# Attention scores of four tiles at once in every second step, with two tiles in one PSUM bank for each head

## The chip, the cores and the metric

The kernel runs on one NeuronCore of a Trainium2 chip. Its time is device time in microseconds (us). TensorE (PE) multiplies matrices and writes only into PSUM, which has eight banks of 512 float32 columns in each of 128 partitions. VectorE (DVE) and ScalarE (ACT) read PSUM; GpSimd (POOL) works on SBUF alone; SyncE (SP) issues most of the DMAs. Each engine works through its own queue of instructions in order and waits on semaphores for the others.

## The reference, cut to what matters

One decoder block on 1024 tokens of width 1024, in float32: a SwiGLU half-step, a mixer, and another SwiGLU half-step. The change touches the attention of the mixer, which has 12 heads of width 64 in three groups of four, with windows and dilations (128, 1), (512, 4) and (2048, 16):

```python
s = jnp.einsum('brnqhd,brnkhd->brnhqk', qb, kk).astype(jnp.float32) * (Dh ** -0.5)
s = jnp.where(allowed[None, None, :, None], s, -jnp.inf)
m = jnp.max(s, axis=-1, keepdims=True)
p = jnp.exp(s - m)
l = jnp.sum(p, axis=-1, keepdims=True)
o = jnp.einsum('brnhqk,brnkhd->brnqhd', p, vv.astype(jnp.float32)) / jnp.swapaxes(l, 3, 4)
```

Beside attention the mixer has a pooling branch, whose last product is `y_pool @ w_branch_pool` (512 by 1024), and both branches are gated and merged.

## The kernel before, in words

Float32 products are made of three products of rounded parts (high by high, high by low, low by high), the parts being held as `fp32r`.

Attention works on 48 **slots**. A slot is one tile of 128 queries of one group for a pair of heads. Each of the six uses (a group for a pair of heads) has eight slots. A slot has either 128 keys (one block) or 256 keys (two blocks); every slot of the group with dilation 16 has one block, in the group with dilation 4 every second slot has one, in the first group only the first slot has one. The order of the uses is: group 0, 1, 2 for the first pair of heads, then 1, 2, 0 for the second.

The main loop has 24 steps, `q` from 0 to 23; step `q` starts two slots, 2q and 2q+1. So steps 0 to 3 and 20 to 23 belong to the first group, 4 to 7 and 12 to 15 to the second, 8 to 11 and 16 to 19 to the third. The loop is under a manual schedule: each engine executes its instructions in the order in which the code writes them. In step `q` the code writes, in this order:

- `scores` (matmuls on line 1552, written tile `s`): for each slot six matmuls, three products for each of two heads. A head contracts over 64 rows, the first head on partitions 0 to 63 and the second on 64 to 127, so these use half of the array each, and two run side by side. Each slot takes two PSUM banks of the tag `mm`, one for each head.
- `trans_p(q - 1)` (L1599, tile `tp`): PE transposes the exponentials of the step before, 128 by 128 at a time: four to eight transposes for two slots, into one or two banks of the tag `acc`.
- `next(fill)` (L1702, tile `yp`): each call issues four 512-column matmuls of the pooling branch; twelve make one output bank (`acc`). The loop has 38 calls from step 2 on: two in a step, and one where `q % 4 == 3`. The two first calls stand in step 1.
- `gather` (L1650): DVE copies the attention output of step q - 3 out of PSUM.
- `masked` (L1570, tile `e`): DVE adds the mask to the scores and finds the maximum: one instruction for each head of each slot, then one that reads the maximum out.
- `values(q - 2)` (L1632, tile `o`): 6 to 12 matmuls of 256 columns that multiply transposed exponentials with values, into one `acc` bank.
- `split_p(q - 1)`: ACT copies the transposed exponentials to the high part (L1611, `ehi`), DVE makes the low part (L1614, `elo`).
- `split_ring` (L1212 on ACT, L1213 on POOL): the queries and keys of the next use are split into high and low parts. Two of these stand in the third step of a use, one in its second and one in its fourth; in the first use two stand in the third and two in the fourth; in the last use and in the first step of each use there is none.
- `end_branches` (L1716): DVE takes a finished pooling bank.
- `exponents` (L1579): ACT takes the exponentials in place, four instructions with an accumulator read after each.
- `house`: DMAs of statistics and values, and late side work.

In steps 18 to 21 the code also transposes weighting factors (`fa`, L1533, banks of the tag `mm`) between `masked` and `values`. PSUM is one pool with four banks of each tag, `mm` and `acc`. The framework gives a bank to a new tile when the instructions that use its old tile are done, and keeps two engines off the same bank at the same time: a reader of a bank waits for the matmuls into it that were written earlier in the code.

Of the kernel before, what the change touches and what calls it, by code (L numbers as in the profile page):

```python
# [16 lines left out]
P = 128  # L17
# [8 lines left out]
HD = 64  # L26
SC = HD ** -0.5
GROUPS = 3
# [8 lines left out]
def tokens(g, i):  # L37

    if g == 0:
        return i * P, 1, (i - 1 if i > 0 else None)  # L40
    if g == 1:
        r, b = divmod(i, 2)
        return r + 4 * P * b, 4, (i - 1 if b else None)
    return i, 8, None
# [74 lines left out]
def three(hi_lo_l, hi_lo_r):  # L119

    lh, ll = hi_lo_l
    rh, rl = hi_lo_r
    return ((lh, rh), (lh, rl), (ll, rh))
# [3 lines left out]
def tile_block(  # L127
# [29 lines left out]
    ve, ac, gp, pe = nc.vector, nc.scalar, nc.gpsimd, nc.tensor  # L157
# [10 lines left out]
    def bank(tag, name):  # L168
        return psum.tile([P, HALF], F32, tag=tag, name=name)
# [1028 lines left out]
    ring = {}  # L1198

    def load_ring(u, tile):  # L1200

        ring[u] = []
        for a in range(2):
            y, hi = tile(F32, f"qk{u}_{a}_in"), tile(F32R, f"qk{u}_{a}_hi")
            nc.sync.dma_start(y, qk_dram[u][a].rearrange("h d c -> (h d) c"))
            ring[u].append((hi, y.bitcast(F32R), y))

    def split_ring(u, n):

        hi, lo, y = ring[u][n // 2]  # L1210
        c = (LOWS, HIGHS)[n % 2]
        ac.activation(hi[:, c], y[:, c], AF.Copy)  # L1212
        gp.tensor_tensor(lo[:, c], y[:, c], hi[:, c].bitcast(F32), op=OP.subtract)  # L1213
# [24 lines left out]
    def load_branch(d):  # L1238
        w, gb = row_part(f"wab{d}"), row(f"gb{d}")
        nc.sync.dma_start(w.rearrange("p (q c) -> p q c", q=2).bitcast(F32), late_w[1 + d][:, :, 256:768])  # L1240
        nc.sync.dma_start(gb, gate_dram[d][:, 1])
        pool_in[d] = (w.rearrange("p (q c) -> p q c", q=2), gb)
# [116 lines left out]
    with tc.manual_schedule():  # L1359
# [4 lines left out]
        for k in range(len(items) + 4):  # L1364
# [6 lines left out]
            if k < len(items):  # L1371
                q, m = items[k]
# [3 lines left out]
            if k - 1 in results:  # L1376
                q, m = items[k - 1]
# [40 lines left out]
    def open_w_o():  # L1418
        wo_pools.append(wo.enter_context(sbuf(f"wo{len(wo_pools)}", "right")))
# [46 lines left out]
    slots = [(hp, g, i) for hp in range(HPAIRS) for g in ((0, 1, 2), (1, 2, 0))[hp] for i in range(NT)]  # L1466
# [30 lines left out]
    def make_factors(hp, eng):  # L1497
        st = stats[hp]
        m, l = st[:, :, :, 0:2], st[:, :, :, 2:4]
        top = att_small.tile([P, 1, NT, 2], F32, name=f"top{hp}")  # L1500
        w = att_small.tile([P, GROUPS, NT, 2], F32, name=f"w{hp}")
        f = att_small.tile([P, GROUPS, NT, 2], F32, name=f"f{hp}")
        every = [P, GROUPS, NT, 2]
        ve.tensor_tensor(top[:, 0], m[:, 0], m[:, 1], op=OP.min)
        ve.tensor_tensor(top[:, 0], top[:, 0], m[:, 2], op=OP.min)
        eng.tensor_tensor(w, top.to_broadcast(every), m, op=OP.subtract)
        yield
        ac.activation(w, w, AF.Exp)
        yield
        eng.tensor_tensor(f, w, l, op=OP.mult)  # L1510
        eng.tensor_tensor(top[:, 0], f[:, 0], f[:, 1], op=OP.add)
        eng.tensor_tensor(top[:, 0], top[:, 0], f[:, 2], op=OP.add)
        ve.reciprocal(top, top)
        eng.tensor_tensor(f, w, top.to_broadcast(every), op=OP.mult)

        f_of[hp] = sums_o.tile([P, GROUPS, NT * 2, HD], F32, tag="f", bufs=1, name=f"f_of{hp}")
        for g in range(GROUPS):
            src = f[:, g].rearrange("p i a -> p (i a)")[:, :, None].to_broadcast([P, NT * 2, HD])
            if hp == 0:
                gp.tensor_copy(f_of[hp][:, g], src)  # L1520
            elif g == 1:
                ve.tensor_copy(f_of[hp][:, g], src)
            else:
                ac.activation(f_of[hp][:, g], src, AF.Copy)
        yield
# [10 lines left out]
    def blocks(g, i):  # L1536

        return 1 if tokens(g, i)[2] is None else 2

    T = {}  # L1540

    def scores(s):
        hp, g, i = slots[s]
        u = hp * GROUPS + g
        n = blocks(g, i)
        ks = slice((i + 1 - n) * P, (i + 1) * P)
        ps = [bank("mm", f"s{s}_{a}")[:, :n * P] for a in range(2)]
        (qhi, qlo, _), (khi, klo, _) = ring[u]
        for j, (l, r) in enumerate(three((qhi, qlo), (khi, klo))):
            for a in range(2):  # L1550
                rows = slice(a * HD, (a + 1) * HD)
                pe.matmul(ps[a], l[rows, i * P:(i + 1) * P], r[rows, ks], start=(j == 0), stop=(j == 2))  # L1552
        T[s] = {"s": ps}

    def masked(s):
        hp, g, i = slots[s]
# [34 lines left out]
    def trans_p(q):  # L1591
        tiles, n = pair(q)
        banks = [bank("acc", f"tp{q}_{j}") for j in range(-(-n // HALF))]
        tp[q] = []
        for s, c0, w in tiles:
            p = banks[c0 // HALF][:, c0 % HALF:c0 % HALF + w] if n <= HALF else banks[s % 2][:, :w]
            e = T[s].pop("e").rearrange("p a c -> p (a c)")
            for j in range(w // P):
                pe.transpose(p[:, j * P:(j + 1) * P], e[:, j * P:(j + 1) * P], ident)  # L1599
            tp[q].append((p, c0, w))  # L1600
        if n <= HALF:
            tp[q] = [(banks[0][:, :n], 0, n)]
# [120 lines left out]
    def send():  # L1723
        while stores:
            nc.sync.dma_start(*stores.pop())

    def branches():
        for n in range(2 * KT):
            yield from branch(n)

    fill = branches()
# [45 lines left out]
    def advance(gen, n=1):  # L1777
        for _ in range(n):
            next(gen, None)
# [24 lines left out]
    with tc.manual_schedule():  # L1804
        load_ring(uses[1], ring_tile)
        load_branch(1)
        factors = [make_factors(hp, eng) for hp, eng in enumerate((gp, ve))]
        combines = [[Combine(hp, half, adds, lower) for half in range(2)]
                    for hp, (adds, lower) in enumerate((((gp, gp), gp), ((gp, ve), ve)))]
        splits = {}  # L1810
        for q in range(N // 2):
            send()
            u, i = divmod(q, NT // 2)
            if 0 < u < len(uses) - 1 and i == 0:
                load_ring(uses[u + 1], ring_tile)
            scores(2 * q)
            scores(2 * q + 1)
            if q == 1:
                next(fill)
                next(fill)  # L1820
            if q > 0:
                trans_p(q - 1)
                splits[q - 1] = split_p(q - 1)
            if q > 1:
                next(fill, None)
                if q % 4 != 3:
                    next(fill, None)
            if q > 2:
                gather(2 * q - 6)
                gather(2 * q - 5)  # L1830
            masked(2 * q)
            masked(2 * q + 1)

            j = q - N // 4 - 6
            fa = [combines[0][j // 2]] * (2 - j % 2) if 0 <= j < 4 else []
            for f in fa:
                f.rows()
            if q > 1:
                values(q - 2)
            if q > 0:  # L1840
                advance(splits[q - 1], 2)
            for n in ((), (0,) if u > 0 else (), (2, 1) if u > 0 else (0, 2), (3,) if u > 0 else (1, 3))[i]:
                if u + 1 < len(uses):
                    split_ring(uses[u + 1], n)
            for f in fa:
                f.product()
            end_branches()
            exponents(2 * q)
            exponents(2 * q + 1)
            house(2 * q)  # L1850
            house(2 * q + 1)
        send()
        right_b.close()
        load_ya(3)
        load_merge(0)
        load_merge(1)
        open_w_o()
        q = N // 2
        trans_p(q - 1)
        splits[q - 1] = split_p(q - 1)  # L1860
        advance(factors[1])
        next(fill, None)
        values(q - 2)
        gather(2 * q - 6)
        gather(2 * q - 5)
        advance(splits[q - 1], 2)
        advance(factors[1], 2)
        next(fill, None)
        end_branches()
        values(q - 1)  # L1870
        for s in range(2 * q - 4, 2 * q):
            gather(s)
        for n in range(8):
            combines[1][n // 4].step()
            if n != 3:
                next(fill, None)
            end_branches()
            send()
            if n == 3:
                load_merge(2)  # L1880
        for k in (3, 4):
            load_merge(k)
# [34 lines left out]
    ops, banks = {}, {}  # L1917
# [66 lines left out]
    with tc.manual_schedule():  # L1984
# [66 lines left out]
        r = [rows_first2(t) for t in range(2)]  # L2051
# [211 lines left out]
```

## Time and profile before

| | |
|---|---|
| median of three runs | 1911.03 us (1910.6 to 1911.14) |
| the profiled execution, own time | 1910.72 us |
| its span | 1908.9 us |
| mean granted TensorE clock | 0.999 |
| PE busy | 99% of the span |
| the attention loop in the profile | about 1044.5 to 1147.4 us |

In a timeline the columns are the start in us, the length in us, the engine, the line, the operation, what it writes and reads, shapes and how many instructions are merged into the row; in brackets stands how long the engine sat idle before and what released it. In the chain of waits a piece begins where the piece before it ended. The matmuls overlap in the pipeline, so the rate of PE is read from the starts of matmuls, not from their lengths.

### The profile page before, as it was taken

To read this page: it belongs to the slowest core of one execution; us is meant where nothing else is said; L and a number is where in the kernel's file an instruction comes from. 1 tells how busy PE (TensorE), PEld (TensorE's weight loads), DVE (VectorE), ACT (ScalarE), POOL (GpSimd) and SP (SyncE) were. 2 spreads that over 40 slices of the span, in tenths; PEclk is the share of its full clock that TensorE was granted. 3 is DMA by queue.
4 is the path that set the end of the run, shared out by engine and by line. 5 is a ranking of instruction groups with operands and counts; after the bars stand their busy time and mean duration, and the time that the engine had idled before them with its cause. 6 is when DMAs were issued, how large, how long until landed. Compare 5 with 4: busy or idle time off the path is not lost.

```text
span 1908.9 us, 24939 instructions
## 1 busy us (share of the span) xinstructions
PE 1896.3 (99%) x8946; PEld 1574.4 (82%) x8946; DVE 1336.5 (70%) x2017; ACT 760.1 (40%) x1364; POOL 732.0 (38%) x548
## 2 busy tenths in 40 slices
PE   9999999999999999999999999999999999999998
PEld 8888888888888887888888888888888888888886
DVE  7786556557776776667875896887665556577777
ACT  6333333333344543334444772353333323333344
POOL 6333333331223355454544455553333333312132
PEclk9999999999999999999999999999999999999999
DMA  4155223336466627655667977643433223454564
GB/s 189 50 194 176 83 88 106 138 116 208 150 234 217 204 92 228 230 215 195 235 223 286 292 247 270 262 152 119 169 116 127 84 88 116 150 192 139 193 221 166
DMA packets 144940, 331.98 MB, mean 174 GB/s; under 512 B 19120, under 2 KB 39856, under 8 KB 143280
## 3 DMA queue, kind: packets, MB, share of 16 engines
q1 hardware_dynamic: 137280, 308.00, 46.9%
q10 hardware_dynamic: 7536, 22.39, 3.2%
q8 instruction: 70, 1.15, 0.3%
q14 instruction: 54, 0.44, 0.1%
HBM read 229.61 MB, written 100.73 MB: 173 GB/s over the span
## 4 chain that ended last, share of the span: by engine, by line
PE 91%; issue 3%; POOL 2%; DVE 2%; ACT 1%; DMA 1%; SPq 0%; POOLq 0%; ACTq 0%; DVEq 0%
PE d_f L754 18%; PE u_mixm L332 16%; PE wo L1954 4%; PE yp L1702 2%; PE o L1632 1%; PE ya L1767 1%; PE s L1552 1%; PE u_f20b L332 1%; PE u_f11a L332 1%; PE u_f20a L332 1%; PE u_f11b L332 1%; PE u_f210b L332 1%; PE u_f210a L332 1%; PE u_f29b L332 1%; PE u_f29a L332 1%
## 5 line engine op out<-in xcount | busy, mean ns | idle before, releaser
L754 PE MATMUL d_f<-bhi_f,ahi_f 128*128 128x512 f32 x616 | 240.4, 390 | 0.0
L754 PE MATMUL d_f<-bhi_f,alo_f 128*128 128x512 f32 x616 | 239.8, 389 | 0.0
L754 PE MATMUL d_f<-blo_f,ahi_f 128*128 128x512 f32 x616 | 239.7, 389 | 0.0
L716 POOL TENSOR_TENSOR alo_f<-g_f,ahi_f 128x512 fp32r<-128x512 f32 x60 | 84.3, 1421 | 293.6 <-ACT ahi_f L712 293.6
L332 PE MATMUL u_mixm<-xhi_t_mix,wc_mixm 128*128 128x512 f32 x608 | 195.2, 392 | 1.2 <-POOL wc_mixm L309 1.1
L332 PE MATMUL u_mixm<-xhi_b_mix,wc_mixm 128*128 128x512 f32 x456 | 148.9, 392 | 0.0
L754 PEld LDWEIGHTS d_f<-bhi_f,alo_f 128*128 128x128 f32 x616 | 115.6, 188 | 24.7 <-DVE alo_f L716 0.4
L332 PEld LDWEIGHTS u_mixm<-xhi_t_mix,wc_mixm 128*128 128x128 f32 x608 | 113.7, 188 | 26.8 <-POOL wc_mixm L309 2.7
L754 PEld LDWEIGHTS d_f<-blo_f,ahi_f 128*128 128x128 f32 x616 | 115.7, 188 | 23.8
L754 PEld LDWEIGHTS d_f<-bhi_f,ahi_f 128*128 128x128 f32 x616 | 115.6, 188 | 23.7 <-DVE xlo_b_mix L411 0.2
L332 PE MATMUL u_mixm<-xlo_t_mix,wc_mixm 128*128 128x512 f32 x304 | 118.4, 389 | 0.0
L309 POOL TENSOR_TENSOR wc_mixm<-s_mixm,wc_mixm 128x512 fp32r<-128x512 f32 x52 | 73.5, 1414 | 101.8 <-ACT wc_mixm L304 101.8
L332 PEld LDWEIGHTS u_mixm<-xhi_b_mix,wc_mixm 128*128 128x128 f32 x456 | 85.6, 188 | 17.7 <-issue 0.3
L304 ACT ACTIVATE wc_mixm<-s_mixm 128x512 fp32r<-128x512 f32 x76 | 47.3, 628 | 125.7 <-DVE s_mixm L364 56.7
L332 PE MATMUL u_mixm<-xlo_b_mix,wc_mixm 128*128 128x512 f32 x228 | 88.8, 389 | 0.0
L712 ACT ACTIVATE ahi_f<-g_f 128x1024 fp32r<-128x1024 f32 x84 | 81.9, 975 | 4.1 <-DMA g_f<-gs_f 4.1
L309 POOL TENSOR_TENSOR wc_mixm<-raw,wc_mixm 128x512 fp32r<-128x512 f32 x40 | 61.0, 1529 | 44.6 <-ACT wc_mixm L304 33.3
L712 ACT ACTIVATE bhi_f<-s_f2w 128x512 fp32r<-128x512 f32 x55 | 32.7, 627 | 96.0 <-DVE s_f2w L732 88.4
L332 PEld LDWEIGHTS u_mixm<-xlo_t_mix,wc_mixm 128*128 128x128 f32 x304 | 57.1, 188 | 11.8
L712 ACT ACTIVATE bhi_f<-s_f1w 128x512 fp32r<-128x512 f32 x55 | 32.9, 630 | 85.1 <-DVE s_f1w L732 80.3
L716 DVE TENSOR_TENSOR alo_f<-g_f,ahi_f 128x1024 fp32r<-128x1024 f32 (+1 forms) x48 | 58.6, 1222 | 7.8 <-ACT ahi_f L712 7.8
L1954 PE MATMUL wo<-w_o,o_hi 128*128 128x512 f32 x224 | 60.2, 391 | 0.0
(1321 smaller groups left out, 5077.6 us busy)
## 6 DMA issues: line engine op xcount, KB each, us to landing
g_f<-gs_f SPq DMA_DIRECT2D x70, 512.0 KB, 4.8
gs_f<-y_f SPq DMA_DIRECT2D x88, 256.0 KB, 3.3
raw<-in_w2a_dram SPq DMA_DIRECT2D x35, 512.0 KB, 3.9
raw<-in_w2b_dram SPq DMA_DIRECT2D x35, 512.0 KB, 4.2
gs_f<-gb_f SPq DMA_DIRECT2D x46, 256.0 KB, 2.3
raw<-in_w1a_dram SPq DMA_DIRECT2D x22, 512.0 KB, 4.8
raw<-in_w3a_dram SPq DMA_DIRECT2D x22, 512.0 KB, 5.6
raw<-in_w1b_dram SPq DMA_DIRECT2D x22, 512.0 KB, 4.3
```

The costliest lines, as they stand in the source:

```text
L304: ac.activation(w[:, 0], src, AF.Copy)
L309: eng.tensor_tensor(w[:, 1], src, w[:, 0].bitcast(F32), op=OP.subtract)
L332: pe.matmul(p, a, b, start=(start and i == 0), stop=(i == 11), skip_group_check=not start)
L712: ac.activation(hi[:, c], src, AF.Copy)
L716: eng.tensor_tensor(lo[:, d], src[:, o], hi[:, d].bitcast(F32), op=OP.subtract)
L754: pe.matmul(self.banks[m][t], l, r, start=(first and q == 0), stop=(last and q == 2))
L1552: pe.matmul(ps[a], l[rows, i * P:(i + 1) * P], r[rows, ks], start=(j == 0), stop=(j == 2))
L1632: pe.matmul(p, l, r, start=(j == 0), stop=(j == end))
L1702: pe.matmul(p, a, b, start=(j == 0), stop=(j == 11))
L1767: pe.matmul(p, a, b, start=(j == 0), stop=(j == 5))
L1954: pe.matmul(banks[m][t], l, r, start=(st == 0 and n == 0), stop=(st == 1 and n == 5))
```

## The change

Scores are now issued only in even steps: `scores(q)` and `scores(q + 1)`, which is the work for slots 2q to 2q + 3. One call takes two `mm` banks, one for each head, and both of its slots lie side by side in them, each in its half of 256 columns. Odd steps issue no scores. The pooling calls are shared out otherwise: from step 2 on, an even step has one, an odd step has two, and steps 5, 9, 13, 17 and 21 have a third one, at the end, after `values` and the split. The number of calls in the loop stays 38. Nothing else moves.

```diff
-    def scores(s):
-        hp, g, i = slots[s]
-        u = hp * GROUPS + g
-        n = blocks(g, i)
-        ks = slice((i + 1 - n) * P, (i + 1) * P)
-        ps = [bank("mm", f"s{s}_{a}")[:, :n * P] for a in range(2)]
-        (qhi, qlo, _), (khi, klo, _) = ring[u]
-        for j, (l, r) in enumerate(three((qhi, qlo), (khi, klo))):
-            for a in range(2):
-                rows = slice(a * HD, (a + 1) * HD)
-                pe.matmul(ps[a], l[rows, i * P:(i + 1) * P], r[rows, ks], start=(j == 0), stop=(j == 2))
-        T[s] = {"s": ps}
+    def scores(q):
+
+        banks = [bank("mm", f"s{q}_{a}") for a in range(2)]
+        for s in (2 * q, 2 * q + 1):
+            hp, g, i = slots[s]
+            u = hp * GROUPS + g
+            n = blocks(g, i)
+            ks = slice((i + 1 - n) * P, (i + 1) * P)
+            c0 = s % 2 * 2 * P
+            ps = [b[:, c0:c0 + n * P] for b in banks]
+            (qhi, qlo, _), (khi, klo, _) = ring[u]
+            for j, (l, r) in enumerate(three((qhi, qlo), (khi, klo))):
+                for a in range(2):
+                    rows = slice(a * HD, (a + 1) * HD)
+                    pe.matmul(ps[a], l[rows, i * P:(i + 1) * P], r[rows, ks], start=(j == 0), stop=(j == 2))
+            T[s] = {"s": ps}
...
-            scores(2 * q)
-            scores(2 * q + 1)
+
+            if q % 2 == 0:
+                scores(q)
+                scores(q + 1)
...
                 next(fill, None)
-                if q % 4 != 3:
+                if q % 2 == 1:
                     next(fill, None)
...
             if q > 0:
                 advance(splits[q - 1], 2)
+            if q > 1 and q % 4 == 1:
+                next(fill, None)
```

## The prediction

> **What bounds the kernel now.** I read the page first, then the attention loop in stretches of 10 us, then who waits there, then the timeline of single steps. In the fence: the span and the engines' busy time from the page, one stretch of the loop (busy us of each engine, granted clock, DMA share, GB/s), and two of the waits (total us, times, longest).
>
> ```profile
> span 1908.9 us, 24939 instructions
> ...
> PE 1896.3 (99%) x8946; PEld 1574.4 (82%) x8946; DVE 1336.5 (70%) x2017; ACT 760.1 (40%) x1364; POOL 732.0 (38%) x548
> ```
> ```profile
> 1084.00:1094.00 10.00, 10.00 (x77) 8.67 (x76) 9.12 (x38) 6.93 (x23) 6.14 (x5) 1.00 0.98 195
> ```
> ```profile
> ACT ehi L1611 <- PE tp L1599: 19.7, 20, 2.1
> ...
> PEld tp L1599 <- ACT e L1579: 1.5, 5, 0.5
> ```
>
> The reader should see that PE is never idle in this stretch and runs at full clock, so PE time that is saved or lost in the loop counts one for one. DVE comes close behind. ACT has room on average, but it waits 19.7 us for transposes: its work hangs on when PE delivers them. PE in turn waits only 1.5 us for exponentials. The change alters that relation.
>
> **What it saves: passages between full and half array.** The timeline of PE in step 11, where two score matmuls (one for each head) make a row, and two places for comparison from the end of the loop and behind it:
>
> ```profile
> 1091.34 0.28 PE L1632 MATMUL o<-ehi,v_in 128*128 128x256 f32 x1
> ...
> 1091.71 0.28 PE L1552 MATMUL s<-qk_in,qk_hi 64*128 64x128 f32 x2
> ...
> 1092.15 0.28 PE L1552 MATMUL s<-qk_hi,qk_in 64*128 64x128 f32 x2
> 1092.36 0.66 PE L1599 MATMUL tp<-ident,e 128*128 128x128 f32 x4
> ...
> 1147.32 0.28 PE L1632 MATMUL o<-ehi,v_in 128*128 128x256 f32 x1
> 1147.44 1.20 PE L1599 MATMUL tp<-ident,e 128*128 128x128 f32 x8
> ...
> 1153.52 0.60 PE L1533 MATMUL fa<-ident,f_of 128*128 128x128 f32 x4
> ```
>
> From the last value matmul to the first transpose it is 1.02 us with scores between (1091.34 to 1092.36), and 0.12 without (1147.32 to 1147.44). Four transposes take 0.66 behind scores and 0.60 behind pooling. So the scores of a step cost 1.02 - 0.12 + 0.06 = 0.96 us. Appended to another block of scores they cost six pairs at their pitch, (1092.15 - 1091.71) / 4 = 0.11, so 0.66. Each odd step saves 0.30. There are eleven from step 3 on (steps 0 and 1 have their scores back to back already): 3.3 us. I add 0.2 for the scores of step 21, which are stretched today in the stretch with `fa`: **3.5 us saved**.
>
> **The opening.** PE and ACT in the first steps:
>
> ```profile
> 1046.45 0.73 PE L1552 MATMUL s<-qk_hi,qk_hi 64*128 64x256 f32 x2
> ...
> 1049.01 0.19 ACT L1579 ACTIVATION_READ_ACCUMULATOR e<-e,stats 128x1 f32 x1
> ...
> 1049.30 0.82 PE L1599 MATMUL tp<-ident,e 128*128 128x128 f32 x6
> ...
> 1051.29 1.91 PE L1599 MATMUL tp<-ident,e 128*128 128x128 f32 x8 [0.27 <-ACT e L1579]
> ...
> 1052.53 0.19 ACT L1579 ACTIVATION_READ_ACCUMULATOR e<-e,stats 128x1 f32 x1
> ```
>
> The stretched score row (0.73) waits for a bank that `masked` empties; with four banks for four slots, the first two steps wait for none. The last row pair shows the price of a wait on exponentials: the transposes end 1053.20, which is 0.48 after the exponentials (1052.72), because the last head's two transposes follow them. So the transposes of step 0 could end 1049.20 + 0.48 = 1049.68 in place of 1050.12: 0.4 gained, and no more, as the exponentials don't move. Those of step 1 wait anyway, eight in 1.91; the scores of step 3, six pairs or 0.7, now fall into that wait. **1.1 us saved.**
>
> **What it costs: the cover of the exponentials.** In an even step ACT's queue holds: copy of the transposes of step q - 1, the ring splits, exponentials of step q. The copy waits for the transposes of q - 1, which stand behind two blocks of scores now. From the end of those transposes PE has one pooling call and `values` before it needs the exponentials of q; before, it had two pooling calls, `values` and a block of scores. ACT's rows of steps 10, 6, 2 and 16 (the last row of each is the end of its exponentials), and the chain of waits, whose pooling pieces start where transposes end:
>
> ```profile
> 1089.10 0.60 ACT L1611 ACTIVATE ehi<-tp 128x512 fp32r<-128x512 f32 x1 [1.17 <-PE tp L1599]
> 1089.62 1.15 ACT L1212 ACTIVATE qk_hi<-qk_in 128x512 fp32r<-128x512 f32 x2
> ...
> 1092.12 0.19 ACT L1579 ACTIVATION_READ_ACCUMULATOR e<-e,own_stats 128x1 f32 x1
> ```
> ```profile
> 1075.46 0.19 ACT L1579 ACTIVATION_READ_ACCUMULATOR e<-e,own_stats 128x1 f32 x1
> ```
> ```profile
> 1056.65 0.19 ACT L1579 ACTIVATION_READ_ACCUMULATOR e<-e,stats 128x1 f32 x1
> ```
> ```profile
> 1114.80 0.19 ACT L1579 ACTIVATION_READ_ACCUMULATOR e<-e,own_stats 128x1 f32 x1
> ```
> ```profile
> 1053.20 1.85 PE yp L1702 x8
> ...
> 1072.22 1.83 PE yp L1702 x8
> ...
> 1109.20 0.92 PE yp L1702 x4
> 1110.12 1.07 PE o L1632 x9
> ...
> 1112.81 1.85 PE yp L1702 x8
> ...
> 1146.17 1.43 PE o L1632 x12
> ```
> ```profile
> 1089.06 1.84 PE yp L1702 x8
> 1090.90 0.71 PE o L1632 x6
> ```
>
> From the end of the transposes of q - 1 to the end of the exponentials of q, with two ring splits: step 10 1092.31 - 1089.06 = 3.25, step 6 1075.65 - 1072.22 = 3.43, step 2 1056.84 - 1053.20 = 3.64. Without a split: step 16 1114.99 - 1112.81 = 2.18, so the pair of splits costs 1.07, and other steps without one take 2.36 (second group) and 2.57 (first).
>
> The cover is 0.92 plus values, less 0.16 (a piece ends 0.28 after its last start, the transposes could start 0.12 after it): 1.47 with six value matmuls, 1.83 with nine, 2.19 with twelve. To it comes the length of the transposes themselves (0.60 for four; 0.82 for six; eight at 0.11 and 0.27 for the last make 1.03), and the exponentials' end plus 0.48 (0.33 where the last head has one transpose) has to fit in. The idle time of PE is the excess:
>
> - step 10: 3.25 + 0.33 - 1.47 - 0.60 = 1.5
> - steps 6 and 14: 3.43 + 0.48 - 1.83 - 0.82 = 1.3 each; step 2: 3.64 + 0.48 - 1.83 - 1.03 = 1.3
> - step 18: as 10, less eight `fa` transposes at 0.11: 0.6
> - step 12: 2.36 + 0.48 - 1.47 - 0.82 = 0.55; step 22: 0.2; steps 8 and 16: 0.1 each; 4 and 20: none.
>
> Together **6.8 us lost**. This falls on TensorE, and everything behind the transposes in its queue moves with it. After an odd step no such wait arises: two or three pooling calls, values and two blocks of scores stand there, at least 1.84 + 0.71 + 0.96 + 0.66 = 4.2 us, against at most 3.25 in the group with so few value matmuls. DMAs and the queues of SP and POOL keep their order; no DMA is moved past another.
>
> **Banks for the values.** In odd steps the transposes (two banks), a finished and a new pooling bank and the values want five of four `acc` banks in step 13 and in step 23, and in 21 for the late call. PE then waits for DVE's low part. DVE in step 14 and the last scores of that step:
>
> ```profile
> 1102.93 1.62 DVE L1650 COPY o<-o 64x128 f32<-64x128 f32 x4 [0.40 <-PE o L1632]
> 1104.58 0.29 DVE L1570 CUSTOM_DVE_ANT_0 e<-s,mask 128x128 f32<-128x128 f32 x1
> ...
> 1105.70 1.02 DVE L1614 TENSOR_TENSOR elo<-tp,ehi 128x256 fp32r<-128x256 f32 x2
> ```
> ```profile
> 1103.50 0.28 PE L1552 MATMUL s<-qk_hi,qk_in 64*128 64x256 f32 x2
> ```
>
> In step 13 DVE frees the first bank about 1.62 + 1.12 + 0.5 (half of the low part) = 3.2 after the values before; PE asks for it after the wait 0.55, transposes 0.6 and two calls 1.84, so at 3.0: 0.2 to 0.3. In step 23 masks and low parts are longer and DVE runs behind: 0.8; in step 21 0.2. I take **1.3 us lost**; the ends are 0 (a bank happens to be free) and 4 (three times until the pooling bank is taken, the low part's 1.02 and more).
>
> **A rule on shared banks.** In the rows just shown, DVE copies outputs until 1104.55, while the step's scores have all started by 1103.50; so DVE's first mask wouldn't start earlier if half of the scores were enough for it. The Trainium skill, in "PSUM — Partial Sum Buffer", section "PSUM bank collisions raise a hardware error", says that two engines must not touch the same bank and quadrant at once, whatever the addresses, so the first slot's mask has to wait for the second slot's scores in that bank. By the rows this costs nothing; by the rule without that cover it is the last rival below.
>
> **The sum.** 6.8 + 1.3 - 3.5 - 1.1 = +3.5 us on the profiled execution's 1910.72, so 1914.2; the median of the runs shown is 0.31 higher: 1914.5. A measurement can tell about 0.2%, here 3.8 us, from no change, so the forecast lies just inside of that bound, with its own range of +1.5 to +6 on both sides of it.
>
> **The rivals.**
> - *The waits don't add up.* While PE waits for exponentials, DVE catches up; then banks are free, and the other small stretched places near `fa` go too: 6.8 - 3.5 - 1.1 - 0.5 = +1.7, so 1912.7. For it: DVE has 0.9 us of 10 idle in the stretch shown. Against it: its waits would have to be where PE's are.
> - *The chain of ACT stays hidden, and the kernel gets faster.* Then only 3.5 + 1.1 remain: 1906.4. It needs 1.3 us more cover in steps 2, 6, 10, 14, or exponentials that don't queue behind the splits; it is decided where the transposes of an even step's slots start without an idle time of PE. For it: PE waits only 1.5 us on exponentials today. Against it: four rows of ACT in a row, in program order, leave no room.
> - *Shared banks bind.* If DVE is free when an even step's scores begin, its mask starts three pairs of each head later, 0.34 us, and the exponentials with it, in twelve even steps: +4.1 on the forecast, 1918.6. It decides itself where the copies (1.62) end before the scores (1.0). Against it: they end later in every step whose rows I read.
>
> **How the numbers follow.** Forecast 0.45, and I split it by the bound as 0.24 slower and 0.21 within it; waits that don't add up 0.25 (within); shared banks 0.20 (slower); hidden chain 0.10 (faster). This gives faster 0.10, within 0.2% 0.46, slower 0.44. The predicted time is the forecast's 1914.5. The range 1909.5 to 1919 leaves out the hidden chain and waits larger than all bounds above.
>
> **What would show it.** Right: PE idle 1.2 to 1.5 us in front of or within the transposes at the start of steps 3, 7, 11 and 15, released by ACT's exponentials, about 7 us in all over 1.5 now; the passage from values to transposes 0.12 in odd steps; scores in blocks of 24 without stretched rows. Wrong: no such idle time; waits of PE for DVE in the score rows; or waits for a bank in front of values that come near those for exponentials.

## The result, and the profile after

The changed kernel takes 1915.07 us (median of 14 runs, 1914.48 to 1915.9) against 1911.03 (14 runs): a ratio of 1.0022, with a 95% interval from 1.0016 to 1.0029. That is 4.0 us slower, inside the range, 0.6 us above the predicted 1914.5, and just on the slow side of the bound of 0.2%. The profiled execution took 1915.86 us with a span of 1913.8, at the same granted clock of 0.999. From the first score matmul to the first matmul behind the loop (`ya`) PE takes 121.0 us, before 117.2, so 3.8 us are lost there. The two profiled executions differ by 4.9 us in span; the other 1.1 lie outside of that stretch, where the code is the same, and the profiled execution of the changed kernel is one of the slowest of its 14.

After the change: the engines' busy time from the page, and three of the waits in the attention loop, two of PE's weight loads (PEld) and one of its matmuls (total us, times, longest):

```profile
PE 1897.0 (99%) x8946; PEld 1572.6 (82%) x8946; DVE 1337.0 (70%) x2017; ACT 759.7 (40%) x1364; POOL 731.2 (38%) x548
```
```profile
PEld tp L1603 <- ACT e L1583: 7.2, 23, 0.7
...
PEld fa L1533 <- DVE stats L1574: 0.9, 1, 0.9
...
PE tp L1603 <- ACT e L1583: 1.0, 4, 0.5
```

The work is the same, but the transposes wait for exponentials 7.2 us on the weight loads, before 1.5, and 1.0 us on the matmuls, before 0.3 (the two overlap in time and don't add up). The waits for DVE's masks in front of `fa` are new. None of this shows in the page's 99%, for one of its 40 slices is 48 us long and has a 9 as long as PE idles less than 4.8 us in it. The windows view tells more; this is the stretch that the prediction showed as wholly busy:

```profile
1084.00:1094.00 10.00, 9.36 (x67) 7.50 (x67) 8.55 (x36) 6.22 (x22) 5.06 (x5) 1.00 1.00 197
```

The timelines of PE and of ACT of the changed kernel around the end of step 10:

```profile
1091.56 0.28 PE L1636 MATMUL o<-ehi,v_in 128*128 128x256 f32 x1
1092.31 1.48 PE L1603 MATMUL tp<-ident,e 128*128 128x128 f32 x4 [0.47 <-ACT e L1583]
1093.55 0.48 PE L1706 MATMUL yp<-xhi_b_mix,wab 128*128 128x512 f32 x1
```
```profile
1090.24 0.60 ACT L1615 ACTIVATE ehi<-tp 128x512 fp32r<-128x512 f32 x1 [2.81 <-PE tp L1603]
1090.74 1.14 ACT L1212 ACTIVATE qk_hi<-qk_in 128x512 fp32r<-128x512 f32 x2
1091.78 0.39 ACT L1583 ACTIVATE e<-e,own_stats 128x128 f32<-128x128 f32 x1
...
1093.22 0.19 ACT L1583 ACTIVATION_READ_ACCUMULATOR e<-e,own_stats 128x1 f32 x1
```

ACT sits idle for 2.81 us, because the transposes it copies stand behind 24 score matmuls; then it runs copy, two ring splits and four exponentials in a row, and PE, which has only one pooling call and six value matmuls meanwhile, waits. The four transposes of step 11 take 1.48 us, one for each head as its exponentials end, where 0.60 would do, and they start 0.75 us after the last value matmul in place of 0.12.

Three more waits of the changed kernel's PE, two for masks in front of `fa`, one for a bank:

```profile
1126.86 0.85 PE L1533 MATMUL fa<-ident,f_of 128*128 128x128 f32 x6 [0.65 <-DVE own_stats L1574]
```
```profile
1135.66 1.09 PE L1533 MATMUL fa<-ident,f_of 128*128 128x128 f32 x8 [0.47 <-DVE stats L1574]
```
```profile
1150.48 0.39 PE L1636 MATMUL o<-ehi,v_in 128*128 128x256 f32 x1 [0.36 <-DVE elo L1618]
```

From the spacing of PE's starts beyond the usual pitch I read the waits from step 3 on:

| wait of PE | predicted, us | measured, us |
|---|---|---|
| transposes for exponentials of steps 2, 6, 10, 12, 14 | 1.3, 1.3, 1.5, 0.55, 1.3 | 1.05, 1.15, 1.46, 0.48, 1.15 |
| the same, steps 8, 16, 18, 22 | 0.1, 0.1, 0.6, 0.2 | 0.06, 0.06, 0, 0.21 |
| `fa` for masks, steps 18 and 20 | none | 0.81, 0.64 |
| banks: steps 13, 21, 23 | 0.25, 0.2, 0.8 | 0.34, 0.27, 0.53 |
| sum | 8.1 | 8.2 |

(The predicted entries add up to 8.2; 8.1 is the sum that the prediction used. Behind each wait for a bank the next start is another 0.1 late, which the table leaves out.) The loop grew by 3.8, so some 4.4 us came back, 4.6 by the prediction. The table shows sizes, not causes. The runs below test those.

### The profile page after: what moved, and what is told of

Read it like the earlier page. It is cut to its first block, busy times and chain, and to the rows that moved or that the text cites. A ratio compares the mean times of both kernels' runs of the same rounds, so it can differ in the third digit from the quotient of the medians.

```text
span 1913.8 us, 24948 instructions
## 1 busy us (share of the span) xinstructions
PE 1897.0 (99%) x8946; PEld 1572.6 (82%) x8946; DVE 1337.0 (70%) x2017; ACT 759.7 (40%) x1364; POOL 731.2 (38%) x548
## 3 DMA queue, kind: packets, MB, share of 16 engines
q8 instruction: 70, 1.15, 0.2%
```

## Experiments

Each was timed beside the kernel before; ratios are to it.

**The scores alone.** The pooling calls are shared out as before, so an even step has two again.

```diff
                 next(fill, None)
-                if q % 2 == 1:
+                if q % 4 != 3:
                     next(fill, None)
...
-            if q > 1 and q % 4 == 1:
-                next(fill, None)
```

> The change with the pooling calls shared out as before (two in an even step, one or two in an odd one). Cover theory: the second call of the even step adds 0.92 us of cover, so the waits for exponentials in the changed kernel's odd steps (1.05, 1.15, 1.46, 0.48, 1.15 us in steps 3, 7, 11, 13, 15) shrink to about 0.1, 0.2, 0.5, 0, 0.2, and the waits of the factor transposes for masks (0.8 and 0.6) go; about 1.9 us of waits stay against 4.6 saved: 1908.3 us, faster than the kernel before by 0.1%. Shared-bank theory (DVE's masks wait for the scores of the second slot in the bank): the sharing out changes nothing, 1914 to 1916. Theory that the passages saved nothing: about 1911 to 1913.

1910.74 us, ratio 1.0000 (0.9991 to 1.0009). One more pooling call in an even step takes the whole loss away, as the cover theory says and the shared-bank theory doesn't. But the gain to 1908.3 failed to come. The waits of steps 3, 7 and 15 shrank to 0.2 each, as expected; that of step 11 rose to 1.9. ACT's timeline of this kernel in step 10 shows why:

```profile
1087.89 0.60 ACT L1615 ACTIVATE ehi<-tp 128x512 fp32r<-128x512 f32 x1 [1.75 <-PE tp L1603]
1089.77 1.15 ACT L1212 ACTIVATE qk_hi<-qk_in 128x512 fp32r<-128x512 f32 x2 [1.28 <-DMA qk_in<-qk]
1090.82 0.39 ACT L1583 ACTIVATE e<-e,own_stats 128x128 f32<-128x128 f32 x1
```

The ring split waits 1.28 us for its load, which SP issued at 1079.0 to 1080.2; and the exponentials wait behind the split. In the kernel before the same split came at 1089.62 without a wait: there SP issued the load 1.0 us later (1079.99), and it was still on time, so it took at least 1.1 us less. Why it is slower here isn't shown; the next large load on SP's queue (`wab`) is issued 2.6 us after it, in the kernel before 3.9. The other half of the missing gain is waits for DVE from step 18 to step 23, about 2 us, where the expectation leaves 0.9 for all waits other than those for exponentials.

**The pooling calls alone.** The kernel before with the calls of the change.

```diff
                 next(fill, None)
-                if q % 4 != 3:
+                if q % 2 == 1:
                     next(fill, None)
...
+            if q > 1 and q % 4 == 1:
+                next(fill, None)
```

> The kernel before with only the pooling calls shared out as in the change. Cover theory: in an even step the cover of the exponentials is one call, values and a block of scores; by the rows of before this is too short by 0.55 us in step 10, 0.3 in 6 and 14 and 0.2 in step 2: +1.3 us, 1912.3, and up to 1913.5 if banks for values are short in odd steps too. If the sharing out costs nothing by itself: 1911.0.

1913.62 us, ratio 1.0014 (1.0005 to 1.0023). Sharing out is a loss by itself, a little above the range that was expected (1912.3 to 1913.5). In the trace the waits for exponentials are about 1.0 us, a bank in step 13 costs 0.3, and `fa` and the scores behind it lose about 1.8 us to waits for DVE, where the scores of the kernel before lose 0.4.

**Ring splits behind the exponentials**, in the changed kernel and in the kernel with the scores alone:

```diff
-            for n in ((), (0,) if u > 0 else (), (2, 1) if u > 0 else (0, 2), (3,) if u > 0 else (1, 3))[i]:
-                if u + 1 < len(uses):
-                    split_ring(uses[u + 1], n)
...
             exponents(2 * q + 1)
+            for n in ((), (0,) if u > 0 else (), (2, 1) if u > 0 else (0, 2), (3,) if u > 0 else (1, 3))[i]:
+                if u + 1 < len(uses):
+                    split_ring(uses[u + 1], n)
```

> The changed kernel with the ring splits moved behind the exponentials of their step on ACT's and POOL's queues. Cover theory: two splits cost 1.07 us of the chain, so the waits in steps 3, 7, 11, 15 fall to about 0, 0.1, 0.4, 0.1; the 0.5 of step 13, the waits of the factor transposes (1.4) and those for banks (1.3) stay: 1911 us, with 1910 and 1912 as ends. Shared-bank theory: the exponentials wait for the masks and not for the splits, so at most a few tenths: 1914.5 or more.

> Scores of four slots in every second step, pooling calls as before and ring splits behind the exponentials. Cover theory: no wait for exponentials is left after the opening, and what remains is the passages saved (3.5 us) and the opening (1.1) less some 0.5 us of waits for banks: 1906.9 us, 0.2% faster than before. If the passages saved nothing: 1910 to 1911. Shared-bank theory: above 1911.

The changed kernel falls to 1911.75, ratio 1.0005 (0.9997 to 1.0014): 3.3 us of its loss hang on where the ring splits stand. The move takes two of them from in front of the exponentials in each of five even steps, and one or two in nine odd steps; a shared bank has no part in that. With the scores alone it is 1911.64, ratio 1.0004 (0.9995 to 1.0012), 4.7 us more than expected. The waits for exponentials are nearly gone, as expected (0.5 us in step 13 stay). In their place stands one of 1.9 us in front of `fa` in step 18. Timelines of this kernel: PE at `fa`, then DVE from the end of step 17, then POOL:

```profile
1123.65 0.52 PE L1533 MATMUL fa<-ident,f_of 128*128 128x128 f32 x3 [1.75 <-DVE own_stats L1574]
```
```profile
1121.07 0.25 DVE L1513 RECIPROCAL top<-top 128x16 f32<-128x16 f32 x1 [2.67 <-POOL top L1512]
1121.24 1.51 DVE L1654 COPY o<-o 64x128 f32<-64x128 f32 x4
1122.78 0.29 DVE L1574 CUSTOM_DVE_ANT_0 e<-s,mask 128x128 f32<-128x128 f32 x1
```
```profile
1118.91 1.28 POOL L1213 TENSOR_TENSOR qk_in<-qk_in,qk_hi 128x512 fp32r<-128x512 f32 x1 [1.62 <-ACT qk_hi L1212]
1120.15 0.29 POOL L1510 TENSOR_TENSOR f<-w,stats 128x48 f32<-128x48 f32 x1
```

POOL's half of the ring split in step 17 now waits for ACT's later half, the sums of the factors stand behind it on POOL, DVE's reciprocal waits 2.67 us for them, and the copies and masks of step 18 stand behind the reciprocal. The same wait in front of `fa` is in the changed kernel with the splits behind (1.94 us). The move was right for the even steps and wrong for step 17.

**Only in even steps**, in the kernel with the scores alone:

```diff
-            for n in ((), (0,) if u > 0 else (), (2, 1) if u > 0 else (0, 2), (3,) if u > 0 else (1, 3))[i]:
+            parts = ((), (0,) if u > 0 else (), (2, 1) if u > 0 else (0, 2), (3,) if u > 0 else (1, 3))[i]
+            for n in parts if q % 2 == 1 else ():
                 if u + 1 < len(uses):
                     split_ring(uses[u + 1], n)
...
             exponents(2 * q + 1)
+            for n in parts if q % 2 == 0 else ():
+                if u + 1 < len(uses):
+                    split_ring(uses[u + 1], n)
```

> Scores of four slots in every second step, pooling calls as before, ring splits behind the exponentials in even steps only, so that POOL's split of step 17 stays ahead of its factor work. Theory that DVE bounds the end of the loop: DVE runs without a gap from the reciprocal of the factors in step 17 to the end of the loop in every version (31.4 us in the kernel before), so what is saved there is given back, and only the opening (1.1 us) and the eight passages before step 18 (2.4 us) count, less 1 to 1.5 us of waits left (values for copies, 0.4 each in steps 6 and 14; transposes in step 13, 0.5): about 1909 us, and the 1.9 us wait of the factor transposes in step 18 goes. Theory that PE alone bounds: 1907.

1910.65 us, ratio 0.9996 (0.9987 to 1.0005). The wait in step 18 fell from 1.9 to 0.3. In the profiles the loop is 1.0 us shorter than before; the expected 1909 did not come, and the trace has scores, pooling and values waiting for DVE about 2 us in steps 20 to 23.

**Copies of outputs on ACT** in steps 19, 21 and 23, in that kernel, in the kernel before and in the changed kernel:

```diff
         for a in range(2):
             r = slice(a * HD, (a + 1) * HD)
-            ve.tensor_copy(own[hp, g][r, cols], p[r, a, :])
+            if s // 2 in (16, 18, 20):
+                ac.activation(own[hp, g][r, cols], p[r, a, :], AF.Copy)
+            else:
+                ve.tensor_copy(own[hp, g][r, cols], p[r, a, :])
```

> The kernel even_behind with the copies of outputs out of PSUM in steps 19, 21 and 23 on ACT in place of DVE (1.6 us less for DVE in each, 4.8 us in all). Theory that DVE bounds the end of the loop: PE's waits for DVE there (0.2 to 0.5 us each on scores, values and pooling banks, about 1.5 us in all) go, and the passages saved behind step 17 count too: 1.5 us less than even_behind. Theory that DVE isn't the bound there: no difference, or slower by the time that ACT is later with its exponentials.

> The kernel before with the same copies on ACT. Its PE waits for DVE by 0.3 us in the scores of step 21 and hardly elsewhere. Both theories: 1910.5 to 1911.2, the control for the run with the copies moved.

> The changed kernel with the same copies on ACT. Cover theory with DVE bounding the end of the loop: the waits for exponentials up to step 15 stay (5.3 us), the waits for DVE in steps 20, 21 and 23 go (0.64, 0.39 and 0.53 us), so 1913.5 us. Theory that all the loss is exponentials: 1915 or more, as ACT has more to do.

1909.26 us, ratio 0.9990 (0.9981 to 0.9999); 1910.20, ratio 0.9994 (0.9985 to 1.0003); 1914.54, ratio 1.0016 (1.0007 to 1.0025). The first is the only version whose interval lies below the kernel before, if only just; it is 1.9 us faster. It gains 1.4 us on `even_behind`, near the expected 1.5. But the control gained about 1.0, more than the 0.7 it was allowed at most, so relief for DVE is worth most of that without the change in the scores, and I can't say that DVE alone holds back what the passages save at the end of the loop. The changed kernel gained 0.5 to 0.9 of the expected 1.5 (0.5 between the medians, 0.9 in the loops of the profiles): its `fa` in step 18 still waits 0.8, and in step 20 0.4 of 0.64.

**The layout alone**: the new `scores`, called in every step of the kernel before.

```diff
-            scores(2 * q)
-            scores(2 * q + 1)
+            scores(q)
```

> The kernel before with only the layout of the change: the two slots of a step share one bank for each head, scores still in every step, pooling calls as before. My reading (the shared bank costs nothing, since DVE copies outputs until after the scores): no loss, and the waits for banks in the first scores (about 0.9 us) and in the scores of step 21 (0.3) go: 1910.0 us, between 1909.7 and 1911.0. Shared-bank theory (the first mask of each step starts 0.34 us later and everything behind it): 1913 to 1919.

1910.91 us, ratio 0.9999 (0.9990 to 1.0008). Two tiles in a bank cost nothing that can be measured: the shared-bank theory's lower end, 1913, is a ratio of 1.0010 and lies just outside of the interval, its upper end, 1919, far outside. The changed kernel's own trace agrees: in the whole loop DVE's masks wait for scores once, for 0.2 us, as often and as long as before. In the trace of the layout alone the first scores wait for no bank. Of the 1.0 us that this gave, 0.6 went back into the transposes of step 0, which follow the exponentials head by head (six in 1.42 us, before 0.82). The loop of the profile is 0.5 us shorter than before, too little for the medians to show.

**More passages**: the kernel before, with the transposes of the first slot between the scores of the two slots.

```diff
             scores(2 * q)
+            half = trans_p(q - 1) if q > 1 else iter(())
+            next(half, None)
             scores(2 * q + 1)
+            advance(half, 2)
...
-                trans_p(q - 1)
```

(`trans_p` now yields after each slot.)

> The kernel before, with the transposes of the first slot of step q - 1 set between the scores of the two slots of step q, from step 2 on: the same instructions, with 22 more passages from transposes to scores and back. By the rows of before a round trip between full and half array costs 0.28 to 0.35 us: +6.2 to +7.7 us, 1917.2 to 1918.9. If the passages cost nothing, and the transposes' own first weights make the gap: below 1913.

1916.83 us, ratio 1.0029 (1.0018 to 1.0041): 5.7 us for 22 more round trips, 0.26 each, a little under the expected 0.28 to 0.35. PE's timeline of this kernel:

```profile
1094.74 0.27 PE L1552 MATMUL s<-qk_hi,qk_in 64*128 64x128 f32 x2
1094.95 0.44 PE L1599 MATMUL tp<-ident,e 128*128 128x128 f32 x2
1095.32 0.33 PE L1552 MATMUL s<-qk_hi,qk_hi 64*128 64x128 f32 x2
```

On both sides of the transposes the starts are 0.2 us apart, where the usual pitch is 0.11, and the second start behind each passage comes another 0.05 late; that is the price, and in this stretch no engine is waited for. So the saving that the change is built on is real.

## Why the prediction was right

*Passages, 3.3 us saved.* Held: the added round trips cost 0.26 each, by which eleven are 2.9 us; I had 0.30 from the rows. (The row of four transposes in 0.60 stands behind values, not behind pooling as the prediction says; that changes no number.)

*The opening, 1.1 us.* Held in its parts: no wait for banks, and the scores of step 3 inside the wait for exponentials. With the layout alone less of it remained, since there the wait in step 1 has nothing to take in.

*Cover of the exponentials, 6.8 us lost.* Held as the cause, in three ways: one more pooling call in even steps takes the loss away, the ring splits moved behind the exponentials take 3.3 of its 4.0 us away, and one call less in the kernel before brings such waits of 1.0 us in. The size was 5.6 where 6.8 stood (the terms as listed add up to 6.95). At the start of steps 3, 7, 11 and 15 it named 1.2 to 1.5 us of idle time, and 1.05 to 1.46 were measured; the steps of the first and the second group have 0.15 to 0.25 less than their terms. In step 18 the wait was not for exponentials: `fa`, which I had counted as cover, waited for the masks itself (0.81), and again in step 20 (0.64). That step of the prediction was wrong. It took `fa` as eight transposes at 0.11 us that always can start, and named what would refute it only in the scores (waits for DVE there).

*Banks, 1.3 us.* Measured 1.1 (1.4 with the late starts behind), in the three steps named, with the low part as the releaser; the shares were off (0.53 in step 23 against 0.8).

*Shared banks cost nothing.* Held, by the layout alone and by DVE's 0.2 us in the changed kernel. Of the rule in the Trainium skill, "PSUM — Partial Sum Buffer", section "PSUM bank collisions raise a hardware error", no run here shows more than that keeping to it was free in this place.

*The number.* That the sum came within 0.6 us is in part luck. The waits for exponentials were put 1.2 us too high, and 1.45 us of waits for masks were not in the sum; the two errors cancel.

*The chance.* The bound of 0.2% ran through the forecast's own range, and 4.0 us lie 0.2 us beyond it; the prediction could not tell these apart.

The rivals: waits that don't add up (1912.7) fell, for PE waited for banks and masks besides the exponentials. The hidden chain (1906.4) fell, too; and when the chain was hidden by hand, 1906.4 was not reached either. That part of the rival was wrong in a way that the prediction didn't see: it took 4.6 us saved on PE as the kernel's gain, while a load (1.28 us late), POOL's factor chain (2.67 us) and DVE (about 2 us) came up behind PE in the versions tried.

What stays open is how the rest of that gain divides between DVE and the chains behind it: the best version has 1.9 of 4.6 us, about 1.0 of which the kernel before gets from the same move of the copies.

## What to carry to other kernels

When work is brought together in every second step, what stood between a producer and its consumer is gone in the other step: count for each step what the in-order queue holds between the two, and compare it with the other engine's chain, instruction by instruction. Here 0.3 us was saved in each pair of steps, and up to 1.5 us of cover was missing. And when the bounding engine gets faster, look for what is late next among loads and side chains: here a saving of 4.6 us met three of them, each worth 1 to 3 us.

## What the runs showed of the hardware that was not expected

A passage of TensorE from full to half array and back cost about 0.26 us here (5.7 us for 22), with starts 0.2 us apart on each side in place of 0.11. Transposes that follow ACT's exponentials head by head start 0.38 us apart (1.48 for four), ACT's own pace, where four in a row take 0.60, so a wait that is spread over the heads costs more than the idle time that its first row shows (0.47).
